# Hybrid decoder layer on one core: four chunks of the second modulation moved to TensorE, a fifth weight slot, a new order of the first loads

## The chip, the cores and the metric

One NeuronCore of a Trainium2 chip runs the whole kernel. The metric is the time of one execution on the device in microseconds (us), as the median of several runs. All data is float32.

## What is computed

One decoder layer on 256 tokens of width 2048. Cut to what matters here:

```python
mod = silu(c) @ w_ada + b_ada                     # (2048) @ (2048 x 12288)
sh1, sc1, g1, sh2, sc2, g2 = split(mod, 6)        # six vectors of 2048
h = rmsnorm(x, norm1_g) * (1 + sc1) + sh1         # first modulation
proj = h @ w_in                                   # 2048 x 4928
o_a = hgrn2(proj)                                 # 8 heads of a gated linear recurrence
o_b = latent_attention(proj)                      # 8 heads, rotary key, low-rank q and kv
x = x + g1 * (concat(o_a, o_b) @ w_out)
h2 = rmsnorm(x, norm2_g) * (1 + sc2) + sh2        # second modulation
y = moe(h2)                                       # top-1 of 4 groups, top-2 of 8 experts, 32 experts
x = x + g2 * y
```

Per expert the weights are 12 MB (gate and up 8 MB, down 4 MB), so the 32 experts are about 403 MB of the 575 MB that a run moves. The six modulation vectors come from one row vector times a 100 MB matrix.

## The kernel before

**The weight stream.** All large weights are cut into chunks of up to 2 MB (128 partitions x 4096 floats). A list `items`, written out in lines 104 to 133, fixes their order, and `ring_fill` (L165) issues their loads in that order on one queue, SyncE's (L174). A chunk takes a slot of a ring; `ring_done` (L183) gives the slot back when the chunk's last reader is done, and only then can the next load go out. The ring has 4 slots (`RING`, L21). Two more are added by `close_temps` (L847, after the second `w_out` chunk of the first half, when the temporaries of the mixers are no longer needed), and one more after the last `w_out` chunk (L892). So 7 chunks at most are loaded ahead of the experts.

**The first modulation.** The vector `c` is copied to all partitions by TensorE (L233, a one-row matmul per 512 columns), passed through sigmoid on ScalarE (L235) and multiplied into `gate` on VectorE (L238). The modulation then comes in two ways. In `ad1_chunk` (L248) and `ada_chunk` (L289) TensorE multiplies a chunk with the silu of `c` as a one-column weight (16 records of the profile per chunk, L257 and L299). In `adt_chunk` (L269) VectorE multiplies a transposed chunk with `gate` and sums along the row: two instructions of 128 x 2048 per chunk (L277). The first 512 features of sh1 and sc1 go through `ad1`, the other twelve blocks of 128 features through `adt` (L106).

**The other modulations** are a list `mods` (L107) of 32 chunks: eight each for g1, for `m2` (the first 1024 features of sh2 and sc2) and for g2, all three on TensorE, then eight chunks `at2` on VectorE for the last 1024 features of sh2 and sc2. `SPREAD` (L23) says how many of them follow each of the last 13 steps: five of the input projection and the mixers, four `w_out` chunks of the first half, four of the second. With `EARLY` one comes before that. So 23 lie ahead of the first `w_out` chunk, three follow it (the last of g2 and two of `at2`), and one follows each of the next six chunks.

**Dense products.** `dense` (L414) handles 128 rows of weights at a time: ScalarE rounds them (L421), VectorE takes the remainder (L422), TensorE does 12 matmuls of 256 columns or their equivalent (L429 to L431, L436 to L438). Four buffers (`NSPLIT`) lie between the engines. `w_out` (L571) adds its result into `xt` on VectorE (L581), and loads `xt` itself, on the same queue as the weights (L588). It is a tile of `arena`, which has 14 buffers; the bias row `brow` of g2, the router weights `wr` and `wr2`, and the mixers' results `mhi` and `mlo` lie in the same arena. The bias is added to g2 on VectorE, row by row (L307), and `gate_rows` (L971) spreads the sum over the partitions.

**Router and experts.** After the last `w_out` chunk come the router (L897 to L966, a chain of small operations), the first gather of tokens (L996) and then the 32 experts (L1052 to L1079), six chunks each.

**The order** of the instructions of each engine is made by a planner from the program's order and priorities; `tc.high_priority(-120)` (L276) puts the VectorE modulation back by 120 steps. The loads of SyncE stand in such an order too: the first chunk of `w_ada` goes out ahead of the four loads of `x` (L214). The table loads of ScalarE (L191 and others) follow the order of its functions.

## Time and profile before

| | us |
|---|---|
| median of 3 runs | 1519.31 |
| lowest, highest | 1517.59, 1519.44 |
| the profiled execution | 1516.6 |
| its span, first to last instruction | 1514.8 |

| engine | busy us | share of the span |
|---|---|---|
| TensorE matmuls | 1116.8 | 74% |
| VectorE | 627.1 | 41% |
| ScalarE | 335.9 | 22% |
| DMA, 574.5 MB at a mean of 379 GB/s | | 91% of 16 engines |

The shares mix two stages. Up to about 580 us all engines work on the mixers while the weights come in; from there on the experts run and TensorE, VectorE and ScalarE mostly wait. The rows below are therefore read by stage. Times in them are microseconds from the start of the span; "x4" is a count of instructions; what stands in brackets is the idle time of the engine just before, and what ended it.

### The profile page before, as it was taken

What the parts mean: (1) busy time and instruction counts of PE and PEld (TensorE: products, weight loads), DVE (VectorE), ACT (ScalarE), POOL (GpSimd) and SP (SyncE); (2) the same over time, 40 slices, a digit from 0 to 9 for tenths busy, and PEclk for the clock granted to TensorE, in tenths of its full rate; (3) what the DMA queues carried; (4) which work ended last, traced back from release to release, by engine and by line L of the source; (5) the groups of instructions that cost most, each with busy time, mean ns of one, the idle gap of its engine ahead of it and who ended that gap; (6) DMA issues with size and microseconds to landing.
All of it is one profiled execution on the core that took longest, in us unless ns stands there. A gap on an engine that the chain in (4) does not pass through costs nothing.

```text
span 1514.8 us, 23373 instructions
## 1 busy us (share of the span) xinstructions
PE 1116.8 (74%) x10141; PEld 708.8 (47%) x10141; DVE 627.1 (41%) x1259; ACT 335.9 (22%) x679; POOL 5.2 (0%) x10
## 2 busy tenths in 40 slices
PE   5979999979888899666666566566667656666665
PEld 2867887637568796333323323323423423333222
DVE  6599998758778862220121122112102112112112
ACT  4734446536433343100100100100100100000000
POOL 0000000000000000000000000000000000000000
PEclk7999999999999998888889888878868889878677
DMA  8789796877979966999999999999999999999995
GB/s 351 270 330 356 300 356 248 333 282 300 373 306 390 389 261 275 427 428 426 427 428 426 427 427 428 426 428 426 427 428 427 427 427 427 427 427 427 427 427 230
DMA packets 42965, 574.52 MB, mean 379 GB/s; under 512 B 4838, under 2 KB 5094, under 8 KB 7660
## 3 DMA queue, kind: packets, MB, share of 16 engines
q1 hardware_dynamic: 41472, 570.51, 90.8%
q10 hardware_dynamic: 1388, 2.49, 0.4%
q8 instruction: 81, 1.33, 0.3%
q14 instruction: 24, 0.20, 0.0%
HBM read 570.88 MB, written 2.10 MB: 378 GB/s over the span
## 4 chain that ended last, share of the span: by engine, by line
DMA 48%; PE 37%; DVE 12%; ACT 2%; issue 1%; ACTq 0%; DVEq 0%
DMA wch<-in_w_gu_dram 37%; DMA wch<-in_w_down_dram 10%; PE pgu L1064 6%; PE pcmb L1019 3%; PE pacc L437 3%; PE pacc L438 3%; PE pacc L431 3%; PE pacc L429 3%; PE pacc L430 3%; DVE wch L277 3%; PE pacc L436 3%; PE py L1042 3%; DVE split L422 2%; PE pada L299 2%; PE pgat L996 1%; DVE proj L461 1%
## 5 line engine op out<-in xcount | busy, mean ns | idle before, releaser
L1064 PE MATMUL pgu<-wch,XT 128*32 128x256 f32 x4096 | 317.2, 464 | 201.3 <-DMA wch<-in_w_gu_dram 201.3
L1064 PEld LDWEIGHTS pgu<-wch,XT 128*32 128x32 f32 x4096 | 141.6, 128 | 368.1 <-DMA wch<-in_w_gu_dram 257.9
L1042 PE MATMUL py<-wch,hT 128*32 128x256 f32 x2048 | 163.2, 474 | 79.3 <-DMA wch<-in_w_down_dram 74.8
L1031 DVE TENSOR_TENSOR hid<-sgu,pgu 128x128 f32<-128x128 f32 x32 | 9.2, 288 | 476.3 <-ACT sgu L1029 476.3
L1046 DVE TENSOR_TENSOR Y<-py,gate 32x256 f32<-32x256 f32 x256 | 107.6, 420 | 213.8 <-PE py L1042 211.0
L421 ACT ACTIVATE split<-wch 128x512 fp32r<-128x512 f32 (+2 forms) x248 | 148.6, 614 | 186.5 <-PE pacc L431 81.4
L422 DVE TENSOR_TENSOR split<-wch,split 128x512 fp32r<-128x512 f32 (+2 forms) x248 | 158.4, 666 | 40.8 <-ACT split L421 38.5
L1042 PEld LDWEIGHTS py<-wch,hT 128*32 128x32 f32 x2048 | 77.8, 130 | 153.0 <-DMA wch<-in_w_down_dram 59.6
L1029 ACT ACTIVATE sgu<-pgu 128x128 f32<-128x128 f32 x32 | 8.9, 278 | 606.9 <-PE pgu L1064 606.9
L1001 ACT ACTIVATE XT<-pgat,sh,a 128x128 f32<-128x128 f32 x128 | 48.2, 457 | 224.9 <-PE pgat L996 224.9
L277 DVE SCALAR_TENSOR_TENSOR wch<-wch,gate 128x2048 f32<-128x2048 f32 x40 | 91.3, 2285 | 0.0
L429 PE MATMUL pacc<-mhi,split 128*128 128x256 f32 x256 | 74.2, 291 | 10.5 <-DVE xt L581 7.2
L437 PE MATMUL pacc<-split,hhi 128*128 128x512 f32 (+1 forms) x192 | 75.1, 391 | 5.9 <-DVE split L422 5.9
L431 PE MATMUL pacc<-mhi,split 128*128 128x256 f32 x256 | 73.5, 289 | 7.9 <-DVE split L422 7.9
L429 PE MATMUL pacc<-hhi,split 128*128 128x256 f32 x256 | 72.6, 287 | 7.7 <-ACT hhi L392 7.2
L436 PE MATMUL pacc<-split,hhi 128*128 128x512 f32 (+1 forms) x192 | 72.3, 389 | 3.0 <-ACT split L421 2.6
L430 PE MATMUL pacc<-hlo,split 128*128 128x256 f32 x256 | 73.1, 287 | 1.7 <-DVE hlo L393 1.7
L431 PE MATMUL pacc<-hhi,split 128*128 128x256 f32 x256 | 72.4, 287 | 2.3 <-DVE split L422 2.3
L430 PE MATMUL pacc<-mlo,split 128*128 128x256 f32 x256 | 73.8, 289 | 0.0
L438 PE MATMUL pacc<-split,hlo 128*128 128x512 f32 (+1 forms) x192 | 73.5, 385 | 0.0
L1019 PE MATMUL pcmb<-Y,pwt 128*128 128x512 f32 x128 | 59.2, 605 | 15.5 <-DVE Y L1046 15.5
L996 PEld LDWEIGHTS pgat<-ohr,x 128*128 128x128 f32 x512 | 63.8, 206 | 9.9 <-issue 9.0
(320 smaller groups left out, 1301.4 us busy)
## 6 DMA issues: line engine op xcount, KB each, us to landing
wch<-in_w_gu_dram SPq DMA_DIRECT2D x128, 2048.0 KB, 31.2
wch<-in_w_down_dram SPq DMA_DIRECT2D x64, 2048.0 KB, 31.8
wch<-in_w_ada_dram SPq DMA_DIRECT2D x28, 2048.0 KB, 10.0
wch<-in_w_ada_t_dram SPq DMA_DIRECT2D x20, 2048.0 KB, 9.8
wch<-in_w_in_dram SPq DMA_DIRECT2D x12, 2048.0 KB, 9.1
wch<-in_w_out_dram SPq DMA_DIRECT2D x8, 2048.0 KB, 14.0
wch<-in_w_in_h_dram SPq DMA_DIRECT2D x8, 1024.0 KB, 9.7
wch<-in_w_in_dram SPq DMA_DIRECT2D x3, 1664.0 KB, 6.7
```

What stands on the lines that cost most here:

```text
L277: V.scalar_tensor_tensor(wk, wk, 1.0, gate, op0=OP.mult, op1=OP.mult, accum_out=r[:, k:k + 1])
L421: S.activation(s[:, 0, :ncol], w, AF.Copy)
L422: V.tensor_sub(s[:, 1, :ncol], w, s[:, 0, :ncol])
L429: PE.matmul(o, s[:, 0, c], hi, start=first and h % 2 == 0, stop=False, skip_group_check=True)
L430: PE.matmul(o, s[:, 0, c], lo, start=False, stop=False, skip_group_check=True)
L431: PE.matmul(o, s[:, 1, c], hi, start=False, stop=stop, skip_group_check=True)
L436: PE.matmul(o, hi[:, c], s[:, 0, :ncol], start=first, stop=False)
L437: PE.matmul(o, hi[:, c], s[:, 1, :ncol], start=False, stop=False)
L438: PE.matmul(o, lo[:, c], s[:, 0, :ncol], start=False, stop=stop)
L1042: PE.matmul(py[32 * j:32 * j + 32, :256], H["T"][:, 32 * kt:32 * kt + 32], w[:, 1024 * kt + 256 * j:1024 * kt + 256 * j + 256], start=kt = ...
L1046: V.tensor_mul(Y[q][r:r + 32, 256 * j:256 * j + 256], py[32 * j:32 * j + 32, :256], gate[32 * j:32 * j + 32, c:c + 256])
L1064: PE.matmul(gu[32 * j:32 * j + 32, :256], XT[G4][kt // 8][:, kt % 8, 32 * e4:32 * e4 + 32], w[:, 1024 * i + 256 * j:1024 * i + 256 * j + 2 ...
```

## The change

- The ring gets a fifth slot (`RING` 5). The room comes from the call that builds the program, which sets `dynamic_dma_scratch_size=1024`.
- Four of the eight `at2` chunks (8 to 11) become four chunks `m3`: the same 512 features of sh2 and sc2, not transposed, multiplied on TensorE in the way of `ada_chunk`, eight matmuls per chunk. After the fourth, ScalarE copies the sums to `rows`, four small matmuls with two selecting columns (`C_SEL`) turn them into columns, and VectorE adds bias and gain for four blocks at once. In `mods` the `m3` chunks stand between `m2` and g2.
- `SPREAD` changes: 25 chunks instead of 23 lie ahead of the first `w_out` chunk, the three that follow it are of g2, and one `at2` chunk follows each of the next four `w_out` chunks. The last three have none. `router_weights(2)` runs after `m3`, so its buffer is taken earlier.
- The remaining `at2` chunks are put back by 20 steps instead of 120.
- The first load of the ring is ordered behind the last load of `x`; five chunks are requested before the constants instead of three.
- `c` and the bias of g2 are rows of one array; `c` is loaded in one transfer instead of two, onto four partitions, and its four one-row matmuls use different row groups of the array. The positions travel with `pcol`, which saves a transfer. `brow` leaves the arena, and its load goes out later.
- The two exponentials of `forget_bound` are ordered behind the load of the logarithm and exponential tables.
- g2 is copied by one ScalarE instruction; the bias is added in `gate_rows` by a second one-row matmul, so there are eight of them instead of four.

The core of the diff:

```diff
-RING, NARENA, NTEMP, NSPLIT, RING2 = 4, 14, (8, 6), 4, 2
-SPREAD = (1, 4, 7, 5, 5, 3, 1, 1, 1, 1, 1, 1, 0)
+RING, NARENA, NTEMP, NSPLIT, RING2 = 5, 14, (8, 6), 4, 2
+SPREAD = (1, 4, 7, 6, 6, 3, 1, 1, 1, 1, 0, 0, 0)
...
-    pos_i = cpool.tile([P, 2], I32, name="pos_i")
     nc.sync.dma_start(pc, A["pcol"])
-    nc.sync.dma_start(pos_i, A["pos"])
...
-    mods = [("ada", b, ch) for b in ("g1", "m2", "g2") for ch in range(8)] + [("at2", kt) for kt in range(8, 16)]
+    mods = [("ada", b, ch) for b, n in (("g1", 8), ("m2", 8), ("m3", 4), ("g2", 8)) for ch in range(n)]
+    mods += [("at2", kt) for kt in range(12, 16)]
...
-            nc.sync.dma_start(t[:, :cols], src)
+            load = nc.sync.dma_start(t[:, :cols], src)
+            if i == 0:
+                in_order(load, ring["behind"])
...
-    crow = tmp([1, 1024], "crow"), tmp([1, 1024], "crow")
-    for h in range(2):
-        nc.scalar.dma_start(crow[h], A["crow"][:, 1024 * h:1024 * h + 1024])
+    crow = big([P, 512], "crow")
+    nc.scalar.dma_start(crow[0:128:32], A["rows"][:, 0])
...
-        nc.sync.dma_start(xx[j], A["xT"][:, 4 * j:4 * j + 4])
-    ring["limit"] = 3
+        x_load = nc.sync.dma_start(xx[j], A["xT"][:, 4 * j:4 * j + 4])
+    ring["behind"] = x_load
+    ring["limit"] = 5
     ring_fill()
-    brow = big([P, 512], "brow")
-    nc.scalar.dma_start(brow[0:128:32], A["b_g"])
     nc.sync.dma_start(cst, A["cst"])
...
-        PE.matmul(ps, one_row, crow[h // 2][:, 512 * (h % 2):512 * (h % 2) + 512], start=True, stop=True)
+        PE.matmul(ps, ones[32 * h:32 * h + 1, :], crow[32 * h:32 * h + 1], start=True, stop=True, tile_position=(32 * h, 0))
...
-            with tc.high_priority(-120):
+            with tc.high_priority(-120 if it[0] == "adt" else -20):
...
+        if b == "m3":
+            for i in range(4):
+                kt = 4 * ch + i
+                for m in range(2):
+                    j, o = 2 * (i % 2) + m, 1024 * i + 512 * m
+                    PE.matmul(acc[b][32 * j:32 * j + 1, :], ca[:, kt:kt + 1], w[:, o:o + 512], start=kt < 2, stop=kt >= 14)
+            ring_done(("ada", b, ch))
+            if ch == 3:
+                S.activation(rows, acc[b], AF.Copy)
+                ps = pm("pcol3")
+                for n in range(4):
+                    PE.matmul(ps[:, 2 * n:2 * n + 2], rows[:, 128 * n:128 * n + 128], cst[:, C_SEL:C_SEL + 2], start=True, stop=True)
+                t = sm(8, "m3")
+                V.tensor_copy(t, ps[:, 0:8])
+                t2 = t.rearrange("p (n b) -> p b n", b=2)
+                mod_shift(sh2[:, 8:12], t2[:, 0], P_BA + 32 + 8, 4)
+                mod_scale(a2[:, 8:12], t2[:, 1], P_BA + 48 + 8, P_N2 + 8, 4)
+            return
...
         if b == "g2":
-            for j in range(4):
-                V.tensor_add(brow[32 * j:32 * j + 1], brow[32 * j:32 * j + 1], acc[b][32 * j:32 * j + 1])
+            S.activation(g2row, acc[b], AF.Copy)
             return
...
-        S.activation(e0, e0, AF.Exp)
-        S.activation(e1, e1, AF.Exp)
+        in_order(S.activation(e0, e0, AF.Exp), tables)
+        in_order(S.activation(e1, e1, AF.Exp), tables)
...
-        ("at2", 11): lambda: router_weights(2),
+        ("ada", "m3", 3): lambda: router_weights(2),
...
-            PE.matmul(ps, ones[32 * j:32 * j + 1, :], brow[32 * j:32 * j + 1], start=True, stop=True, tile_position=(32 * j, 0))
+            for row in (g2row, brow):
+                PE.matmul(ps, ones[32 * j:32 * j + 1, :], row[32 * j:32 * j + 1], start=row is g2row, stop=row is brow,
+                          tile_position=(32 * j, 0))
...
-    nc = bacc.Bacc("TRN2", target_bir_lowering=False, num_devices=1)
+    nc = bacc.Bacc("TRN2", target_bir_lowering=False, num_devices=1, dynamic_dma_scratch_size=1024)
```

## Rows read from the trace of the kernel before

**Rows 1.** The page's head: the span.
```profile
span 1514.8 us, 23373 instructions
```

**Rows 2.** Windows by stage: each engine's busy time (count), granted clock, DMA share, GB/s.
```profile
40.00:240.00 200.00, 184.05 (x1100) 153.44 (x1098) 176.47 (x294) 100.92 (x183) 0.00 (x0) 0.99 0.83 316
240.00:433.00 193.00, 177.91 (x1205) 120.01 (x1205) 141.77 (x293) 98.56 (x188) 2.87 (x3) 0.96 0.76 300
433.00:560.00 127.00, 108.62 (x879) 105.81 (x876) 102.86 (x178) 43.41 (x69) 0.95 (x1) 0.93 0.89 364
560.00:580.00 20.00, 16.55 (x116) 13.68 (x116) 8.54 (x48) 10.03 (x27) 0.00 (x0) 0.74 0.23 93
580.00:1500.00 920.00, 601.57 (x6727) 302.57 (x6727) 166.44 (x378) 64.25 (x185) 0.00 (x0) 0.84 1.00 423
```

**Rows 3.** Timeline of SyncE's queue, 510 to 590: start, duration of the merged stretch, load, count.
```profile
510.74 28.33 SPq L174 DMA_DIRECT2D wch<-in_w_gu_dram  x4
539.16 13.26 SPq L174 DMA_DIRECT2D wch<-in_w_down_dram  x2
556.40 31.56 SPq L174 DMA_DIRECT2D wch<-in_w_gu_dram  x4
```

**Rows 4.** Chain that ended last: start, duration, what; the first and the last expert load.
```profile
578.01 1.86 PE pgu L1064 x32
...
1458.04 30.81 DMA wch<-in_w_gu_dram
```

**Rows 5.** Windows of three shorter stretches, columns as in rows 2.
```profile
40.00:60.00 20.00, 20.00 (x129) 14.65 (x128) 8.46 (x15) 14.59 (x25) 0.00 (x0) 1.00 0.55 181
450.00:460.00 10.00, 2.86 (x12) 2.57 (x13) 9.79 (x21) 2.19 (x4) 0.00 (x0) 0.54 0.99 418
1000.00:1200.00 200.00, 132.72 (x1445) 65.31 (x1437) 35.63 (x78) 12.93 (x38) 0.00 (x0) 0.83 1.01 427
```

**Rows 6.** Timeline of the start, and the four one-row matmuls of `gate_rows` at 563.90.
```profile
2.54 7.16 PE L233 MATMUL pc<-crow,one_row 1*128 1x512 f32 x8 [2.54 <-DMA crow<-in_crow_dram]
...
10.16 1.28 ACT L235 ACT_TABLE_LOAD   x1
...
12.07 1.28 ACT L191 ACT_TABLE_LOAD   x1
13.36 2.00 ACT L327 ACTIVATE sq<-x 128x1024 f32<-128x1024 f32 x2
...
34.33 0.80 PE L429 MATMUL pacc<-hhi,split 128*128 128x256 f32 x2 [7.01 <-ACT hhi L392]
...
563.90 2.27 PE L975 MATMUL pg<-brow,ones 1*128 1x512 f32 x8
```

**Rows 7.** Timeline of VectorE: the first `adt` instruction of the run.
```profile
66.46 2.29 DVE L277 SCALAR_TENSOR_TENSOR wch<-wch,gate 128x2048 f32<-128x2048 f32 x1
```

**Rows 8.** Timeline of ScalarE: its three longest waits for a weight chunk.
```profile
214.57 2.19 ACT L421 ACTIVATE split<-wch 128x512 fp32r<-128x512 f32 x4 [5.06 <-DMA wch<-in_w_in_dram]
...
281.93 2.19 ACT L421 ACTIVATE split<-wch 128x512 fp32r<-128x512 f32 x4 [4.62 <-DMA wch<-in_w_in_dram]
...
450.11 2.19 ACT L421 ACTIVATE split<-wch 128x512 fp32r<-128x512 f32 x4 [9.09 <-DMA wch<-in_w_out_dram]
```

**Rows 9.** Timeline: one TensorE modulation chunk; the bias additions; two successive weight splits.
```profile
445.67 1.90 PE L299 MATMUL pada<-wch,ca 128*1 128x512 f32 x16
447.63 2.78 DVE L307 TENSOR_TENSOR brow<-brow,pada 1x512 f32<-1x512 f32 x4 [1.32 <-PE pada L299]
...
547.92 0.63 ACT L421 ACTIVATE split<-wch 128x512 fp32r<-128x512 f32 x1 [0.79 <-PE pacc L431]
549.35 0.63 ACT L421 ACTIVATE split<-wch 128x512 fp32r<-128x512 f32 x1 [0.79 <-PE pacc L431]
```

**Rows 10.** Groups by line: the VectorE modulation, all 20 chunks.
```profile
L277 DVE SCALAR_TENSOR_TENSOR wch<-wch,gate 128x2048 f32<-128x2048 f32 x40 | 91.3, 2285 | 0.0
```

**Rows 11.** Waits of SyncE's queue up to 620: the loads of `xt`.
```profile
SPq L588 <- PE pacc L431: 6.2, 1, 6.2
```

More of the change, by code (lines that the diff above doesn't have):

```diff
@@ L31 @@
 NEG = -3.0e38
-C_ID, C_TRI64, C_TRI, C_MASK, C_IOTA, C_IOTM, C_FREQ, C_RESET = (
-    0, 128, 256, 384, 640, 672, 704, 736)
-C_W = 992
+C_ID, C_TRI64, C_TRI, C_MASK, C_IOTA, C_IOTM, C_FREQ, C_RESET, C_SEL = (
+    0, 128, 256, 384, 640, 672, 704, 736, 992)
+C_W = 994
 P_C, P_N1, P_N2, P_QA, P_KVA, P_QN, P_KN, P_HO, P_AO, P_LB, P_BA = (
     0, 16, 32, 48, 52, 54, 55, 56, 57, 58, 74)
-P_W = 154
+P_POS = 154
+P_W = 156
 R_QPE, R_KPE, R_B = 0, 64, 128
@@ L133, in tile_hybrid_layer, with in_order, log_exp_tables @@
     index = {it: i for i, it in enumerate(items)}
+    def in_order(inst, before):
+        tc.add_manual_dep(inst.ins, before.ins.name, mybir.DependencyInfo(mybir.DependencyClass.NoSync, mybir.DependencyReason.DATA),
+                          reason="order")
+    def log_exp_tables(inst):
+        load = S.preload_act_table_set("natural_log_exp_and_others")
+        in_order(load, inst)
+        return load
     def source(it):
@@ L145, in source @@
         if k == "ada":
+            if it[1] == "m3":
+                return A["w_ada_3"][it[2]], 4096
             return A["w_ada"][("g1", "m2", "g2").index(it[1]), it[2]], 4096
         if k == "at2":
-            return A["w_ada_t2"][it[1] - 8], 4096
+            return A["w_ada_t2"][it[1] - 12], 4096
         if k == "win":
@@ L186, in ring_done @@
         ring_fill()
-    def log_exp_tables(inst):
-        load = S.preload_act_table_set("natural_log_exp_and_others")
-        tc.add_manual_dep(load.ins, inst.ins.name, mybir.DependencyInfo(mybir.DependencyClass.NoSync, mybir.DependencyReason.DATA),
-                          reason="tables")
     def rsqrt(ms, n):
@@ L228, in tile_hybrid_layer @@
     V.tensor_mul(ca, ca, cin)
-    one_row = cpool.tile([1, P], F32, name="one_row")
-    V.memset(one_row, 1.0)
     for h in range(4):
         ps = pm("pc")
-        PE.matmul(ps, one_row, crow[h // 2][:, 512 * (h % 2):512 * (h % 2) + 512], start=True, stop=True)
+        PE.matmul(ps, ones[32 * h:32 * h + 1, :], crow[32 * h:32 * h + 1], start=True, stop=True, tile_position=(32 * h, 0))
         g = gate[:, 512 * h:512 * h + 512]
@@ L236, in tile_hybrid_layer @@
         if h == 3:
-            log_exp_tables(i)
+            tables = log_exp_tables(i)
         V.tensor_mul(g, g, ps)
+    brow = cpool.tile([P, 512], F32, name="brow")
+    S.dma_start(brow[0:128:32], A["rows"][:, 1])
     acc = {}
     rows = cpool.tile([P, 512], F32, name="rows")
+    g2row = cpool.tile([P, 512], F32, name="g2row")
     sh1 = cpool.tile([P, 16], F32, name="sh1")
@@ L1173, in _layout @@
     sh1, sc1, g1, sh2, sc2, g2 = range(6)
-    L["pcol"] = ac(np.concatenate([L["pcol"]] + [col(ba[k]) for k in (sh1, sc1, sh2, sc2, g1)], axis=1))
-    L["crow"] = np.asarray(i["c"]).reshape(1, D)
-    L["b_g"] = ac(ba[g2].reshape(4, 512))
+    L["pcol"] = ac(np.concatenate([L["pcol"]] + [col(ba[k]) for k in (sh1, sc1, sh2, sc2, g1)]
+                              + [ac(np.asarray(i["positions"])[0].reshape(2, P).T).view(np.float32)], axis=1))
+    L["rows"] = ac(np.stack([np.asarray(i["c"]).reshape(4, 512), ba[g2].reshape(4, 512)], axis=1))
     wt = lambda b: wa[:, :, b].reshape(D, 16, P).transpose(1, 2, 0)
     L["w_ada_t"] = np.stack([wt(sh1), wt(sc1)], axis=2).reshape(16, P, 4096)[4:]
-    L["w_ada_t2"] = np.stack([wt(sh2), wt(sc2)], axis=2).reshape(16, P, 4096)[8:]
+    L["w_ada_t2"] = np.stack([wt(sh2), wt(sc2)], axis=2).reshape(16, P, 4096)[12:]
+    t = np.stack([wa[:, :, b, 1024:1536].reshape(4, 4, P, 512) for b in (sh2, sc2)], axis=3)
+    L["w_ada_3"] = ac(t.transpose(0, 2, 1, 3, 4)).reshape(4, P, 4096)
     t = np.stack([wa[:, :, b, :512].reshape(2, 8, P, 2, 256) for b in (sh1, sc1)], axis=4)
```

4 lines of the change are left out of this document (2 added, 2 removed).

## The prediction

> **What bounds the kernel now.** I read the windows by stage first, because the page's shares mix two programs. From about 580 us to the end the DMA engines are busy all the time at 423 GB/s on average (427 in the middle), while TensorE works 602 of 920 us and VectorE 166 [rows 2, 5]. So the end is set by a stream of weights at a constant rate, and the only question is when that stream begins and how much is already loaded by then. SyncE's queue answers the second: four gate-up chunks and two down chunks go out up to 552, one more at 556.40, and then the queue has no slot [rows 3]; between 560 and 580 the DMA share is 0.23 [rows 2]. So seven chunks are loaded when the first expert chunk is used up, at 578.01 + 1.86 = 579.9 [rows 4]. There are 32 x 6 = 192 chunks of 2.097 MB; the other 185 take 2.097 / 0.427 = 4.91 us each [rows 5], 908.4 us together, which gives 1488.3. The last gate-up load landed at 1458.04 + 30.81 = 1488.9 [rows 4]. The rest, to 1514.8, is a tail that the change leaves alone [rows 1]. The formula therefore holds:
>
> span = (time T1 at which the first expert chunk is used up) + 4.91 x (192 - chunks loaded by then) + 26.5
>
> Up to T1 the engines set the pace. From 40 to 240 both TensorE (184 of 200) and VectorE (176) are nearly full, from 240 to 433 TensorE is (178 of 193), and DMA has a share of 0.83 and 0.76 [rows 2]. From 433 to 560, the `w_out` stage, TensorE works 109 of 127 us, VectorE 103, and DMA's share rises to 0.89 [rows 2]: nothing is full there, the three wait for each other.
>
> **The change part by part**, against the profiled execution (1516.6; its span 1514.8).
>
> *Fifth slot, after T1: -4.9.* Eight chunks loaded instead of seven. It counts in full only if the eighth can land before T1; between 560 and 580 the DMA engines are idle for 0.77 x 20 = 15.4 us [rows 2], so a T1 that is earlier by some 10 us does not take that away (the w_out stage would also have fewer bytes, since two modulation chunks leave it). This term I hold for the surest. The Trainium skill ("DMA: Bandwidth & Descriptors", Specifications) gives a core's limit from HBM as about 358 GB/s. The window at 427 contradicts it for this core [rows 5]; by the page's figure a slot would be an estimated 5.9 us instead of 4.9. The measurement decides.
>
> *The start: -5.0.* ScalarE's squares of `x` begin at 13.36, and the first dense matmul starts at 34.33 after a chain through them [rows 6]. Ahead of the squares stand the four one-row matmuls (7.16 us) and two table loads of 1.28 that the new order saves: one back to the sigmoid at 10.16, one forth again at 12.07 [rows 6]. Tables alone give 2.6. Four one-row matmuls in different row groups exist in this trace, in `gate_rows`: 2.27 us instead of 7.16 [rows 6], so at most 4.9 more. Together 2.6 to 7.5; I take the middle, since sigmoids still follow one another on ScalarE. `x` in front of the first 2 MB chunk lands up to 4.9 us earlier, so it doesn't hold the squares. The chunk now lands later, but what the first dense step needs is `x` and the first two chunks of `w_ada`, 6.3 MB in either order, 14.7 us of transfer at 427: both orders have it by about 20 us, before the chain through `x` is done. The saved transfers of a few KB are worth nothing visible: cover is the 2 MB behind them.
>
> *40 to 240: -4.0.* From 40 to 60 TensorE is full and VectorE works 8.5 of 20 us [rows 5], because the first `adt` chunk is only there at 66.46 [rows 7]; afterwards VectorE is almost the bound (176 of 200). One more slot brings that chunk one load earlier, so one chunk's VectorE work, 2 x 2.285 = 4.6 us [rows 10], can move into the idle time. ScalarE's wait of 5.06 at 214.57 for a chunk [rows 8] may go too. Bounds: nothing (TensorE goes on as the bound) to 8, half of TensorE's idle 16 us in this stretch [rows 2].
>
> *240 to 433: +2.0.* Two more modulation chunks lie ahead of `w_out`: 2 x 1.90 = 3.8 us of TensorE [rows 9], and the end of `m3`, a copy and small operations, that I put at 1 us from the copy of 128 x 512 at 0.63 that ScalarE does in the splits [rows 9]. TensorE is idle 15 us of this stretch [rows 2], and the wait of 4.62 at 281.93 for a chunk [rows 8] may disappear with a deeper ring. Bounds +4.8 to -4.6; I take +2 since the idle pieces lie in dependent chains which only partly admit a filler.
>
> *433 to 560: -11.5.* TensorE needs 64 splits' worth of matmuls at 549.35 - 547.92 = 1.43 us [rows 9], 91.5 us. Lost are 127 - 108.6 = 18.4 us of idle time, and, with a granted clock of 0.93 on average, that is about 18 us at the lower of the two levels (1.2 instead of 2.4 GHz), I estimate some 5 us of slow matmuls after the idle pieces [rows 2]. The largest piece is 450 to 460: 7.1 us idle, clock 0.54, VectorE full [rows 5]. Three things meet there: ScalarE waited 9.09 us for the second `w_out` chunk [rows 8], VectorE did the bias rows for 2.78 us [rows 9], and two `at2` chunks of 2 x 2.285 us each [rows 10]. All three go: the slot loads the chunk earlier, ScalarE copies g2, and three g2 chunks stand in place of one and two `at2`. I count 7.1 + 2.5 for this. The other 11.3 us of idle time I put down to VectorE, which at one `at2` chunk per `w_out` chunk has 4.6 for it, 8 splits that I put at ScalarE's 0.63 each [rows 9], and the additions to `xt`: 9.7 and more, against TensorE's 8 x 1.43 = 11.4, with little room for an instruction at the wrong place; with eight `at2` chunks cut to four, half of it goes, 5.6. Two further g2 chunks cost 3.8 of TensorE. 7.1 + 2.5 + 5.6 - 3.8 = 11.4. Bounds: 3.3 (only the 7.1 less the 3.8) to 19 (18.4 + 5 less 3.8). The later place of the remaining `at2` chunks, 20 steps back instead of 120, has no row; I give it nothing, with up to 2.3 us either way, one instruction ahead of a split.
>
> *560 to T1: 0.* `gate_rows` gets four more matmuls, 2.3 us by its row [rows 6]; they stand while the router's small operations run, where TensorE is idle 3.45 of 20 us [rows 2]. Without that cover they cost 2.3.
>
> Sum: -4.9 - 5.0 - 4.0 + 2.0 - 11.5 = -23.4; T1 comes at about 561. 1516.6 - 23.4 = 1493.2. The profiled execution lies 2.7 below the median of the runs shown, so the median should be 1496.
>
> **The rivals.**
>
> *The start is swallowed.* From 60 to 240 VectorE's work is fixed (176 of 200 us busy), and it begins when the first `adt` chunk lands. If the load order, not the start of the dense steps, sets that moment, then -5 and -4 both end in TensorE waiting for VectorE: 1496 + 9 = 1505. For it: VectorE's load in rows 2. Against it: loads wait for slots there (share 0.55 from 40 to 60 [rows 5]), and an earlier first step frees them earlier.
>
> *VectorE goes on setting the pace in the w_out stage.* Four chunks still need 2 x 2.285 each there, beside splits that TensorE needs every 1.43; if the order keeps an `at2` in front of the splits each time, only the piece at 450 returns, 3.3 instead of 11.5: 1504.
>
> *More is gained.* If TensorE runs without a gap in the w_out stage (-19) and 40 to 240 gives 8, then 1496 - 7.5 - 4 = 1484.5.
>
> *Only the slot counts.* The saved VectorE time is idle time elsewhere and the added chunks cost 4.8: 1516.6 - 4.9 + 4.8, by the median about 1519.
>
> *Slower: the arena blocks the load queue.* SyncE's queue is strictly in order; in the kernel before, the load of the fourth `xt` held it for 6.2 us until a `w_out` matmul was done [rows 11]. By my count 14 buffers were full then: eight of mixer results, `brow`, `wr`, one `wr2` and three `xt`; the change takes `brow` out but fetches the second `wr2` before `w_out` begins, so it again reaches 14 with the third `xt`. If one more tile is alive than I count, two further loads of `xt` wait, each for about one `w_out` chunk (11.4 us), with all weight loads behind them: +22.8, and the gain of 11.5 in that stage is gone as well. 1496 + 22.8 + 11.5 = 1530. It decides as soon as the second `xt` finds no buffer; only its count of 13 speaks against it.
>
> **How the numbers follow.** Forecast 0.52, with a range of its own from 1489 to 1503. Start swallowed 0.16; VectorE goes on 0.14; more gained 0.08; only the slot 0.04; slower 0.06. All but the last two, and these near the edges of what the bounds allow, lie between 1482 and 1511: the upper end is 1496 + 9 + 8, less 2 because both misses in full are unlikely together, the lower end that of the third rival with 2.5 for the start's upper bound. What a measurement of this kernel can tell from no change is about 0.2%, 3 us. Faster: 0.52 + 0.16 + 0.14 + 0.08 = 0.90; same 0.04; slower 0.06.
>
> **What would show it.** The stream after T1 still at 427 with eight chunks requested before T1, T1 at 561; squares beginning near 8 to 9 and the first dense matmul near 29; the first `adt` before 60; `w_out` beginning near 426 and its stage 115 us long, without ScalarE's wait of 9 us and without a low clock at its start; no wait of an `xt` load over 6 us. It would be wrong if DMA never idles before T1 (then the slot is worth nothing), if TensorE waits for `adt` after 200, or if a modulation chunk keeps TensorE waiting for its load between 380 and 430.

## The result and the profile after

| | before | after |
|---|---|---|
| median, us | 1519.31 | 1527.34 |
| lowest, highest | 1517.59, 1520.07 | 1525.05, 1529.43 |
| the profiled execution, its span | 1516.6, 1514.8 | 1527.34, 1525.1 |

The changed kernel is slower by about half a per cent: the ratio of the times is 1.0055, with a 95% interval from 1.0039 to 1.0071. The forecast was 1496, and faster.

The windows by stage of the changed kernel, columns as in rows 2 (busy time and count of TensorE, weight load, VectorE, ScalarE, GpSimd; granted clock; DMA share; GB/s):

```profile
40.00:240.00 200.00, 184.67 (x1091) 156.78 (x1093) 176.85 (x300) 100.41 (x174) 0.00 (x0) 0.97 0.81 313
240.00:433.00 193.00, 171.25 (x1158) 118.26 (x1150) 142.08 (x298) 100.25 (x196) 3.76 (x4) 0.97 0.75 296
433.00:560.00 127.00, 113.12 (x911) 99.95 (x910) 81.22 (x147) 45.08 (x72) 0.00 (x0) 0.95 0.88 364
560.00:580.00 20.00, 18.02 (x147) 16.89 (x145) 9.99 (x41) 8.62 (x22) 0.00 (x0) 0.95 0.57 211
580.00:1500.00 920.00, 603.56 (x6743) 306.43 (x6746) 166.07 (x387) 67.79 (x194) 0.00 (x0) 0.84 0.99 419
...
1000.00:1200.00 200.00, 127.64 (x1440) 63.25 (x1432) 37.81 (x83) 12.35 (x36) 0.00 (x0) 0.86 1.01 427
```

VectorE was relieved between 433 and 560 as planned (81.2 us instead of 102.9 [rows 2]), and the experts' stream is the same as before, 427 GB/s in the middle (the last line, and rows 5). But from 240 to 433, where more work was to be done, TensorE did less, 171.3 instead of 177.9. So the kernel had fallen behind there, and that is where to look.

Four points of the trace, in us from the span's start, place the loss. A split is the preparation of 128 weight rows, rounded on ScalarE and the remainder taken on VectorE; on VectorE the 185th is the first of `w_out`, the 248th is the last; T1 is the end of the first expert chunk, in the changed kernel this line of TensorE's timeline:

```profile
592.95 1.93 PE L1091 MATMUL pgu<-wch,XT 128*32 128x256 f32 x32
```

| | before | after | difference |
|---|---|---|---|
| 169th split | 352.6 | 352.0 | -0.6 |
| first `w_out` split | 431.7 | 445.2 | +13.5 |
| last `w_out` split | 551.4 | 562.7 | +11.3 |
| T1 | 579.9 | 594.9 | +15.0 |
| span | 1514.8 | 1525.1 | +10.3 |

Up to 352 the two kernels are level. Some 14 us are lost from there to the first `w_out` split, 2 come back in the `w_out` stage, nearly 4 are lost in the router, and the fifth slot returns 5 behind T1.

SyncE's queue shows the first of these losses. Each line is the start of a stretch, its length and the chunks requested in it; first the kernel before, then the changed one:

```profile
376.52 0.33 SPq L174 DMA_DIRECT2D wch<-in_w_in_dram  x1
...
409.02 0.33 SPq L174 DMA_DIRECT2D wch<-in_w_out_dram  x1
```

```profile
339.12 31.14 SPq L187 DMA_DIRECT2D wch<-in_w_ada_dram  x5
377.12 0.33 SPq L187 DMA_DIRECT2D wch<-in_w_in_dram  x1
382.42 30.86 SPq L187 DMA_DIRECT2D wch<-in_w_ada_dram  x6
436.53 0.33 SPq L187 DMA_DIRECT2D wch<-in_w_out_dram  x1
```

The first load of `w_out` goes out at 436.53; in the kernel before it went out at 409.02. The queue isn't short of bandwidth: in the window from 420 to 430 the DMA engines are idle (DMA share 0.01; before, 0.27).

```profile
420.00:430.00 10.00, 9.57 (x59) 7.07 (x60) 6.08 (x13) 1.83 (x4) 0.95 (x1) 0.77 0.01 2
```

It waits for slots that modulation chunks hold. These are the queue's waits for a modulation matmul (sum, count, longest), up to 620 in the kernel before and up to 640 in the changed one:

```profile
SPq L174 <- PE pada L299: 142.0, 24, 20.3
```

```profile
SPq L187 <- PE pada L325: 128.0, 23, 23.2
...
SPq L613 <- PE pacc L456: 9.6, 1, 9.6
```

The sum didn't grow, and a wait of some 20 us for matmuls behind the recurrence stood in the queue before too, from 411.1 to 431.4. But it held up the two `at2` chunks then, with `w_out`'s first load already out; with two more chunks ahead it holds up `w_out`'s load itself, from 413.3 to 436.5.

The `w_in` load, by contrast, is only 0.6 us later than before (377.12 against 376.52), and it has landed at 386.13. Yet ScalarE rounds that chunk's first 128 rows 10 us later than before. First the kernel before, then the changed one, where the attention's last exponentials (L842) stand ahead:

```profile
385.48 2.19 ACT L421 ACTIVATE split<-wch 128x512 fp32r<-128x512 f32 x4 [0.68 <-DMA wch<-in_w_in_dram]
```

```profile
391.73 0.51 ACT L842 ACTIVATE s<-s,sm 128x256 f32<-128x256 f32 x1 [6.18 <-DVE sm L840]
...
395.62 0.61 ACT L446 ACTIVATE split<-wch 128x512 fp32r<-128x512 f32 x1
```

So at this place it is the planner's order, and not the date of the load, that differs from the kernel before. In the waits above, the last line is the load of `xt`, of which my slower rival spoke: one wait, 9.6 instead of 6.2 [rows 11], not three.

### The profile page after: what moved, and what is told of

Its sections match the earlier page's. It is cut to its first block, busy times and chain, and to the rows that moved or that the text cites. A ratio compares the mean times of both kernels' runs of the same rounds, so it can differ in the third digit from the quotient of the medians.

```text
span 1525.1 us, 23510 instructions
## 1 busy us (share of the span) xinstructions
PE 1125.5 (74%) x10221; PEld 714.7 (47%) x10221; DVE 607.4 (40%) x1231; ACT 337.1 (22%) x681; POOL 5.1 (0%) x10
## 5 line engine op out<-in xcount | busy, mean ns | idle before, releaser
L454 PE MATMUL pacc<-mhi,split 128*128 128x256 f32 x256 | 74.5, 291 | 13.3 <-DVE xt L606 10.3
L285 DVE SCALAR_TENSOR_TENSOR wch<-wch,gate 128x2048 f32<-128x2048 f32 x32 | 72.9, 2283 | 0.0
L1023 PEld LDWEIGHTS pgat<-ohr,x 128*128 128x128 f32 x512 | 62.7, 203 | 11.1 <-issue 11.1
```

The lines of the kernel that those rows point to most:

```text
L285: V.scalar_tensor_tensor(wk, wk, 1.0, gate, op0=OP.mult, op1=OP.mult, accum_out=r[:, k:k + 1])
L454: PE.matmul(o, s[:, 0, c], hi, start=first and h % 2 == 0, stop=False, skip_group_check=True)
```

## The experiments

All runs were compared with runs of the kernel before on the same chip, in five rounds. "T1" and the splits are read in each run's profiled execution, and one such execution can lie up to 6.6 us from its kernel's median (the start alone: 1526.96 against 1520.39); the verdicts go by the ratios.

### Taking the change apart

**Only the fifth slot**, the rest as before:

```diff
-RING, NARENA, NTEMP, NSPLIT, RING2 = 4, 14, (8, 6), 4, 2
+RING, NARENA, NTEMP, NSPLIT, RING2 = 5, 14, (8, 6), 4, 2
-    nc = bacc.Bacc("TRN2", target_bir_lowering=False, num_devices=1)
+    nc = bacc.Bacc("TRN2", target_bir_lowering=False, num_devices=1, dynamic_dma_scratch_size=1024)
```

> The kernel before with the fifth slot alone. Theory A (the slot is worth one chunk of the stream and no more, 4.9 us; the loss of the whole change comes from the four m3 chunks and their place): about 1514.5. Rival B (more loads ahead change the planner's order so that modulation chunks come before the second recurrence's matmuls, whatever m3 does): the first expert chunk is used up later than at 580, and the time is 1519 or more.

1511.03 us, ratio 0.9945 (0.9927 to 0.9963): a gain of 8 us by the median. Theory A gave the slot 4.9; my sum had 4.9 for it behind T1 and, with the earlier `adt` chunk, 4.0 ahead of it.

**The changed kernel with four slots** (`RING` 4):

> The changed kernel with four slots again. Theory A: the stream starts with seven chunks instead of eight, +4.9 us, 1532. Rival B (the slot itself lets modulation chunks crowd in front of w_out): the w_out stage begins earlier than at 445 and the time is below 1527.

1540.15 us, 1.0134 (1.0112 to 1.0156): without the slot all the rest costs 20 us, and the slot is worth 13 in the changed kernel. That is more than either theory said.

**Only the new start**: the order of `x` and `w_ada`, `c` on four partitions, the table loads, the positions in `pcol`, five requests ahead of the constants.

> The kernel before with the new start alone: x ahead of w_ada, c in one transfer and row groups, exponentials behind the table load, positions with pcol. My prediction: 5 us less, 1514. Theory A (TensorE has the first modulation chunk's matmuls, which wait for the later landing of that chunk, between the two matmuls of the square sums): the first dense matmul 1 to 2 us earlier, nothing left of it at 240, within 2 us of 1519.

1520.39 us, 1.0017 (1.0007 to 1.0027): worth nothing, rather a little less than that.

**No `m3`**: the changed kernel with all eight `at2` chunks and the old `SPREAD`; slot, start and `g2row` stay.

```diff
-    mods = [("ada", b, ch) for b, n in (("g1", 8), ("m2", 8), ("m3", 4), ("g2", 8)) for ch in range(n)]
-    mods += [("at2", kt) for kt in range(12, 16)]
+    mods = [("ada", b, ch) for b, n in (("g1", 8), ("m2", 8), ("g2", 8)) for ch in range(n)]
+    mods += [("at2", kt) for kt in range(8, 16)]
-SPREAD = (1, 4, 7, 6, 6, 3, 1, 1, 1, 1, 0, 0, 0)
+SPREAD = (1, 4, 7, 5, 5, 3, 1, 1, 1, 1, 1, 1, 0)
...
```

> The changed kernel without m3: eight at2 chunks on VectorE and SPREAD as in the kernel before; the slot, the start and the g2 row stay as changed. Theory A (m3 and the two further chunks ahead of w_out cost more than VectorE's relief gives): 1512 to 1516, that is the slot alone (1511) plus about 4 for the eight one-row matmuls, less up to 1.5 for the start. Rival E (the loss comes from the start or from another part kept here): 1523 or more.

1510.69 us, 0.9958 (0.9945 to 0.9970); first `w_out` split at 430.5. So the loss comes with `m3` or with the two chunks that `SPREAD` puts ahead of `w_out`, and without them hardly anything is left but the slot's gain.

### `m3`, or the two chunks ahead of `w_out`?

Two kernels complete the square. The first is the changed kernel with the old `SPREAD` (23 chunks ahead) and `m3`:

> The changed kernel with the old SPREAD alone: the four m3 chunks stay, and 23 modulation chunks stand ahead of w_out instead of 25, two more behind it. Theory E (the two extra chunks, which hold the slots while w_out's loads should start, cost the time): first w_out split 445 -> 431 to 434, last logits matmul at 553 to 557, median 1510 to 1515. Theory F (the m3 chunks themselves cost it, by the planner's order of TensorE's queue and the clearing of the one accumulator): first w_out split not before 440, median 1520 to 1526.

The second has no `m3`, but the new `SPREAD` (25 ahead):

> The opposite half: no m3 chunk (eight VectorE chunks at2, as before), but 25 modulation chunks ahead of w_out as in the changed kernel. The fifth slot, the new start and g2row stay. Theory E: first w_out split at 440 to 446, later than the 430.5 of the kernel without m3 and with 23; median 1518 to 1527. Theory F: first w_out split near 432, median 1510 to 1513.

| median, us (ratio) | 23 ahead of `w_out` | 25 ahead |
|---|---|---|
| eight `at2` | 1510.69 (0.9958) | 1535.16 (1.0115) |
| four `m3`, four `at2` | 1511.99 (0.9962) | 1527.34 (1.0055) |

With 23 chunks it makes no difference whether the four chunks run on TensorE or on VectorE. With 25 both kernels lose, by 15 and 24 us, the one without `m3` more than either theory had expected. So the loss comes with the `SPREAD` line, with or without `m3`. SyncE's queue of the kernel with `m3` and 23 chunks shows the other course:

```profile
337.21 27.82 SPq L187 DMA_DIRECT2D wch<-in_w_ada_dram  x4
368.03 0.33 SPq L187 DMA_DIRECT2D wch<-in_w_in_dram  x1
375.23 26.57 SPq L187 DMA_DIRECT2D wch<-in_w_ada_dram  x5
407.38 0.33 SPq L187 DMA_DIRECT2D wch<-in_w_out_dram  x1
```

One modulation chunk fewer stands ahead of the last `w_in` chunk, which goes out 9.1 us earlier (368.03 instead of 377.12), and one fewer ahead of `w_out`, which goes out 29 us earlier. The recurrence of the last heads needs that `w_in` chunk, and here ScalarE rounds its first rows at 383.56, ahead of the last exponentials (390.31), as in the kernel before. Its first matmuls, L549, in this kernel and then in the changed one (TensorE's timeline):

```profile
415.88 1.94 PE L549 MATMUL ptr<-cst,d 128*128 128x128 f32 x8 [6.84 <-DVE d L542]
428.52 5.33 PE L325 MATMUL pada<-wch,ca 128*1 128x512 f32 x48
435.74 1.06 PE L592 MATMUL pmt<-cst,o 128*128 128x128 f32 x8
```

```profile
420.43 1.86 PE L325 MATMUL pada<-wch,ca 128*1 128x512 f32 x2 [7.54 <-ACT d L537]
422.22 1.97 PE L549 MATMUL ptr<-cst,d 128*128 128x128 f32 x8
...
434.59 6.19 PE L325 MATMUL pada<-wch,ca 128*1 128x512 f32 x56
440.86 1.06 PE L592 MATMUL pmt<-cst,o 128*128 128x128 f32 x8
```

Seen from L592, the mixer's last result, the changed kernel is 5.1 us behind (and 1.8 behind the kernel before, 439.10); at the last split it is 14.3 behind (562.7 against 548.4). What differs most is the work done ahead of that result: eight splits of `w_out` had begun on ScalarE ahead of it in the kernel before and five with `m3` and 23 chunks, but none in the changed kernel.

The kernel without `m3` loses by another course. Its `w_out` load goes out at 414.47, 22 us earlier than in the changed kernel, and its first `w_out` split still comes at 445.7. The 25th chunk is an `at2` chunk there, and VectorE runs its two instructions (at 437.98 and 440.26) ahead of the mixer's last large operations, which began at 438.24 in the changed kernel (L585). L592, which waits for them, starts at 445.96:

```profile
414.47 0.33 SPq L187 DMA_DIRECT2D wch<-in_w_out_dram  x1
```

```profile
437.98 2.28 DVE L285 SCALAR_TENSOR_TENSOR wch<-wch,gate 128x2048 f32<-128x2048 f32 x1
...
443.33 1.23 DVE L585 TENSOR_TENSOR o<-o,sm 128x1024 f32<-128x1024 f32 x1
```

A late load of `w_out` is thus not needed for the loss.

### Number, place, or bytes?

**24 chunks**: `SPREAD` (1, 4, 7, 5, 6, 3, 1, 1, 1, 1, 1, 0, 0), one of the two extra chunks, behind the last `w_in` load.

> The changed kernel with 24 modulation chunks ahead of w_out: five ahead of the last two heads' w_in load, as with 23, and six between that load and w_out's first, as in the changed kernel. Theory E1 (each of the two extra chunks costs by its own place): w_in's load is issued near 368, as with 23, w_out's first load later than 407; first w_out split between 430 and 440, median 1514 to 1522. Theory E2 (only the chunk ahead of the w_in load hurts, since it moves the recurrence): median 1511 to 1514. Theory E3 (only the chunk just ahead of w_out hurts): 1523 to 1528.

1517.99 us, 0.9997 (0.9988 to 1.0005). The `w_in` load is issued at 368.57 and L549 starts at 416.42, as with 23; the last `w_out` split comes at 552.4. So this one chunk costs 6 us by the median, and the other, ahead of the `w_in` load, 9: 1512.0, 1518.0, 1527.3 (5 and 9 by the ratios).

**25 chunks, the extra two early**: (1, 6, 7, 5, 5, 3, 1, 1, 1, 1, 0, 0, 0).

> The changed kernel with 25 chunks ahead of w_out, but the two extra ones right behind the first group of the third mixer (1, 6, 7, 5, 5) instead of around its last w_in load. If the place decides, the last part runs as with 23 chunks: first w_out split at 425 to 432, median 1510 to 1515. If the number decides (two chunks, 9.8 us of stream, ahead of everything that follows), first w_out split at 437 to 447 and median 1520 to 1528.

1533.66 us, 1.0107 (1.0092 to 1.0122), beyond both expectations. An earlier place is no cure, it is worse: the last `w_in` load goes out at 378.59, L549 starts at 427.29, the first `w_out` split at 450.3.

**Fewer ahead of `w_out`**: (1, 4, 7, 6, 3, 3, 2, 2, 1, 1, 1, 0, 0), 22 chunks, but still six ahead of the last `w_in` load.

> The changed kernel with three modulation chunks fewer ahead of w_out: SPREAD (1, 4, 7, 6, 3, 3, 2, 2, 1, 1, 1, 0, 0). Theory A (six chunks in a row hold all five slots, so the first w_out load goes out at 436 instead of 409, the DMA engines stand still from 420 to 437, and the w_out stage then runs behind the stream): the first w_out load goes out 10 to 20 us earlier, the stage ends 8 to 12 us earlier, 1516 to 1519. Rival C (what counts is TensorE's wait of 7.5 us at 413 to 420 for a cleared accumulator): that wait stays, and the time stays within 3 us of 1527.

1516.32 us, 0.998 (0.997 to 0.999). Three chunks were moved behind `w_out`'s start, and 11 us came back; the first `w_out` split is at 422.1 and the stage from there to the last is 130 us long instead of 117.5. The mixer's last result comes at 440.68, as late as in the changed kernel (440.86), but five splits of `w_out` had begun on ScalarE ahead of it; so the lateness of the mixer is not what cost these 11 us. In the kernel with the slot alone, one chunk fewer (`SPREAD` (1, 4, 7, 5, 4, 3, 2, 1, 1, 1, 1, 1, 0)) was no help either:

> The kernel before with the fifth slot alone and one modulation chunk fewer ahead of w_out (22). The kernel with the slot alone took 1511.0 with 23. If 23 already delays w_out's first load, 22 gives a further 2 to 5 us (1506 to 1509); if the stage behind is then limited by the stream, the chunk costs there what it saves here: 1510 to 1513.

1514.58 us, 0.9975 (0.9964 to 0.9986), against 1511.03 with 23, above both values that were expected. Its profiled execution, 1508.94, was the fastest of seven, which is why the median is used. Of the numbers tried, 23 is the best.

**The bytes away**: the first five g2 chunks load 512 of their 4096 columns.

```diff
+            if it[1] == "g2" and it[2] < 5:
+                return A["w_ada"][2, it[2]][:, :512], 512
             return A["w_ada"][("g1", "m2", "g2").index(it[1]), it[2]], 4096
...
-                o = D * k + 512 * j
+                o = 0 if b == "g2" and ch < 5 else D * k + 512 * j
```

> The changed kernel in which the first five g2 chunks, those that stand ahead of w_out's first load, bring only 512 of their 4096 columns each, and their matmuls use these 512 throughout: the same instructions, slots and order, 5 x 7/8 x 2.097 MB = 9.2 MB less to load, 21.5 us of the stream at 427 GB/s; most of the gate's values are others. Theory S (the chunks cost through the slots that they hold until TensorE's queue reaches them, behind the recurrence): w_out's first load is issued at 430 to 437, first w_out split at 441 to 446, median 1523 to 1528. Rival B (they cost through their bytes): w_out's first load before 420, first w_out split before 432, median under 1513.

1529.93 us, 1.0067 (1.0048 to 1.0086). SyncE's queue and two windows of this kernel:

```profile
377.65 0.33 SPq L189 DMA_DIRECT2D wch<-in_w_in_dram  x1
...
437.11 0.33 SPq L189 DMA_DIRECT2D wch<-in_w_out_dram  x1
```

```profile
400.00:410.00 10.00, 9.25 (x64) 8.37 (x64) 8.70 (x17) 8.15 (x11) 0.00 (x0) 1.00 0.06 19
410.00:420.00 10.00, 3.42 (x30) 1.70 (x28) 10.00 (x24) 4.02 (x5) 0.00 (x0) 0.92 0.10 34
```

The median is 2 us above what either theory gave. The DMA engines stand nearly still (0.06 and 0.10), yet the `w_in` and the `w_out` load go out within 0.6 us of the changed kernel's, and nothing is gained. The extra chunks don't cost bytes; they cost their places: in the load queue, where `w_out`'s load waits for a slot and the slot for a matmul behind the recurrence, and, as the kernel without `m3` showed, in the engines' queues.

### One wait after the other

**The accumulator cleared by ScalarE.** The 7.54 us that TensorE waits at 420.43 end with VectorE's clearing of the one accumulator, from 419.84 to 420.32, which stands behind the recurrence's operations (the view names L537, which ended earlier, at 420.04). Here g2's accumulator is cleared by ScalarE.

```diff
-            V.memset(acc[b], 0.0)
+            if b == "g2":
+                S.activation(acc[b], cst[:, 0:512], AF.Copy, scale=0.0)
+            else:
+                V.memset(acc[b], 0.0)
```

> The changed kernel, with the accumulator of g2 cleared by ScalarE instead of VectorE, where the clearing stands behind five large operations of the recurrence. Rival C: TensorE's wait of 7.5 us goes, the recurrence's transposes start near 416 instead of 422, and the time falls by 5 to 7 us, to 1521. Theory A: the wait goes, but the loads of w_out come little earlier because the same six chunks stand ahead of them; the time falls by 3 us or less.

1527.16 us, 1.0061 (1.0042 to 1.0081): no gain. The wait fell to 1.35 us, slots came free earlier and `w_out`'s first load went out at 414.45 instead of 436.53, which Theory A had not expected. The recurrence gained little: its first matmuls came at 420.45 instead of 422.22, now behind a wait of 3.50 for VectorE. But ScalarE splits the chunk only when its queue comes to it, and there the split stands behind the mixer's last result (L501 is the changed kernel's L498):

```profile
441.40 1.27 ACT L501 ACTIVATE mhi<-pmt,pc 128x512 fp32r<-128x512 f32 x2 [4.14 <-PE pmt L595]
442.56 2.19 ACT L449 ACTIVATE split<-wch 128x512 fp32r<-128x512 f32 x4
```

In the kernel with `m3` and 23 chunks, splits of `w_out` stand ahead of it:

```profile
430.20 1.14 ACT L446 ACTIVATE split<-wch 128x512 fp32r<-128x512 f32 x2
...
436.40 1.27 ACT L498 ACTIVATE mhi<-pmt,pc 128x512 fp32r<-128x512 f32 x2 [0.26 <-PE pmt L592]
```

So a late load is not the whole cause here either: the planner's order has also put `w_out`'s first splits behind the mixer. In the changed kernel itself the first split waits only 1.75 us for its load, from 442.80 to 444.55.

**The `at2` chunks put back by 120 steps again** (instead of 20):

> The changed kernel with all VectorE modulation put back by 120 steps, the four at2 chunks too. Theory A (the w_out stage follows its loads, which go out late): within 3 us of 1527. Rival D (put back by 20 steps only, two at2 chunks run one after the other ahead of an xt addition at 507 to 512, and TensorE waits 8.3 us for it): the wait goes and the time falls by 6 to 8 us, to 1520.

1526.10 us, 1.0056 (1.0043 to 1.0069): no effect. But Rival D was not put to the test: the two `at2` instructions stand one after the other ahead of the addition to `xt` as they did (506.60 and 508.81, the addition at 511.80), and TensorE still waits 8.35 us for it.

**VectorE's additions in the slot's kernel**: one addition of the whole accumulator to a cleared `brow` instead of four rows.

> The kernel before with the fifth slot and, in the w_out stage, one VectorE addition of the whole accumulator to brow instead of four additions of a row each (brow cleared first on GpSimd). My prediction gave VectorE's time in the w_out stage a worth. If VectorE sets the pace there, 1 to 2 us less than 1511.0; if not, 1510.5 to 1511.5.

1510.17 us, 0.9947 (0.9932 to 0.9962), against 0.9945 with four: 2 us less on VectorE in the `w_out` stage are worth nothing.

**Half of the `at2` loads.** The four `at2` chunks, all in the `w_out` stage, load half their columns, and VectorE does the same work.

```diff
-            return A["w_ada_t2"][it[1] - 12], 4096
+            return A["w_ada_t2"][it[1] - 12][:, :2048], 2048
...
-            wk = w[:, 2048 * k:2048 * k + 2048]
+            wk = w[:, 2048 * k:2048 * k + 2048] if it[0] == "adt" else w[:, :2048]
```

> The changed kernel in which each of the four at2 chunks, all in the w_out stage, loads only its first 2048 columns, which VectorE multiplies twice: the same instructions, 4 MiB less to load in that stage, and half of those modulation values are others. One chunk of 2 MiB takes 4.91 us in the steady stream, so 9.8 us of transfer are taken out. Theory (the stream is the bound between the first w_out split and the first expert chunk): last VectorE split 562.7 -> 551 to 555 and median 1515 to 1519. Rival (VectorE or TensorE sets the pace there): last split within 3 us of 562.7, median 1524 to 1528.

The total, 3066 us, can't be read, which I hadn't foreseen: the other modulation values change the routing, and the router falls into the path for too many tokens per expert, which loads all experts' weights again (975 MB instead of 574.5). Up to 560 the trace can be read: the last split comes at 556.7, between the two expectations. Of 9.8 us of transfer 6.0 came back, 1.1 of it ahead of the first `w_out` split (1.0 already at the 113th split, long before the edit acts), so the stream sets part of this stage and not all of it. In the changed kernel the DMA share is 1.01 from 445 to 520; from 540 TensorE is full:

```profile
445.00:460.00 15.00, 15.00 (x127) 12.24 (x128) 5.64 (x11) 4.27 (x8) 0.00 (x0) 1.00 1.01 430
460.00:480.00 20.00, 16.97 (x131) 14.76 (x124) 13.07 (x23) 7.73 (x13) 0.00 (x0) 0.91 1.01 426
480.00:500.00 20.00, 18.05 (x139) 17.88 (x139) 14.84 (x26) 7.21 (x12) 0.00 (x0) 0.91 1.01 425
500.00:520.00 20.00, 11.65 (x88) 11.48 (x87) 15.69 (x28) 4.57 (x8) 0.00 (x0) 0.83 1.01 426
...
540.00:560.00 20.00, 20.00 (x169) 19.67 (x169) 13.78 (x23) 9.24 (x14) 0.00 (x0) 1.00 0.46 176
```

### The router, and a candidate

**Four gate matmuls again**: GpSimd clears `brow`, VectorE adds it to `g2row` in one instruction.

```diff
...
             S.activation(g2row, acc[b], AF.Copy)
+            V.tensor_add(g2row, g2row, brow)
...
-            for row in (g2row, brow):
-                PE.matmul(ps, ones[32 * j:32 * j + 1, :], row[32 * j:32 * j + 1], start=row is g2row, stop=row is brow, ...)
+            PE.matmul(ps, ones[32 * j:32 * j + 1, :], g2row[32 * j:32 * j + 1], start=True, stop=True, tile_position=(32 * j, 0))
```

> The changed kernel with the bias of g2 added by one VectorE instruction again, and four one-row matmuls in gate_rows instead of eight. Theory A (the extra matmuls stand in TensorE's queue in front of the router's transposes and the first gather, and cost about 4 us there): from the last w_out matmul to the first expert chunk 21 to 22 us instead of 25; the time falls by 3 to 5 us, to 1523. Rival (they lie beside the router's small operations): within 1 us of 1527.

1524.26 us, 1.0047 (1.0032 to 1.0062); by the ratios 0.0008, some 1 us, better than the changed kernel, with intervals that overlap. Its trace has the 3.8 us: from the last logits matmul to T1 it takes 21.4 instead of 25.2. In the changed kernel the bias's one-row matmuls stand in TensorE's queue ahead of the router's own (L986) and of the gather (L1023):

```profile
580.84 2.07 PE L1001 MATMUL pg<-brow,ones 1*128 1x512 f32 x2
582.84 0.37 PE L986 MATMUL prm<-cst,sm 128*1 128x128 f32 x1
583.14 2.07 PE L1001 MATMUL pg<-g2row,ones 1*128 1x512 f32 x2
585.01 1.91 PE L1001 MATMUL pg<-brow,ones 1*128 1x512 f32 x2
586.85 6.17 PE L1023 MATMUL pgat<-ohr,x 128*128 128x128 f32 x32
```

With it, without `m3` and with 23 chunks:

> The candidate: the changed kernel without m3, with 23 chunks ahead of w_out, and with the bias added to g2row by one VectorE instruction, so that gate_rows has four matmuls instead of eight. Against the kernel without m3 (1510.7) the router's chain should be 3 to 4 us shorter: median 1507 to 1509. If that chain is covered by the loads, no difference: 1510 to 1511.

1511.92 us, 0.9959 (0.9947 to 0.9971): no better than without it (0.9958). The fastest kernels are all the same to within their intervals, 0.9945 to 0.9962: the slot alone, the slot with one addition, and the changed kernel with 23 chunks ahead of `w_out`, with or without `m3`.

## Why the prediction was wrong

By the spans, 1525.1 came where 1491.4 was forecast (1514.8 - 23.4). Of these 33.7 us, 8.4 were missing by the 169th split (-0.6 where the start and 40 to 240 had been booked with -9), 12.1 from there to the first `w_out` split, 9.3 in the `w_out` stage and 3.7 in the router. Behind T1 the forecast held to 0.2.

**The formula: right.** span = T1 + 4.91 x (192 - chunks loaded) + 26.5 gives 594.9 + 903.4 + 26.5 = 1524.8 for the changed kernel; its span was 1525.1. With four slots (T1 604.6, seven chunks) it gives 1539.4 against 1538.4, with `m3` and 23 chunks (579.5) 1509.4 against 1508.6, with the early 25 (600.5) 1530.4 against 1530.6. The largest miss is the kernel with 22 chunks and six ahead of `w_in`: 1514.3 against 1517.5. The slot's -4.9 behind T1 held. Alone the slot is worth 8, near the 4.9 and 4.0 that I had booked for it, and in the changed kernel 13. By the figure of the Trainium skill ("DMA: Bandwidth & Descriptors", Specifications), about 358 GB/s for each of the two cores that share a stack, a chunk would take an estimated 5.9 us. Here one core runs the kernel, and the window from 1000 to 1200 after the change again has 427.

**The start, -5: wrong.** The pieces came at least as large as priced, and none reached the end. The squares began at 5.33 instead of 13.36, the one-row matmuls took 2.08 for three of four, the table loads were gone. But TensorE's queue had this order:

```profile
16.73 1.19 PE L361 MATMUL pss<-sq,ones 128*128 128x256 f32 x2 [7.01 <-DVE lbc L434]
17.85 3.59 PE L265 MATMUL pad<-wch,ca 128*1 128x512 f32 x16
21.37 0.87 PE L361 MATMUL pss<-sq,ones 128*128 128x256 f32 x2
...
32.89 0.80 PE L454 MATMUL pacc<-hhi,split 128*128 128x256 f32 x2 [7.05 <-ACT hhi L417]
```

A modulation chunk of 16 records stands between the two halves of the sum of squares (L361), so the second half began at 21.37, where in the kernel before the whole sum began at 21.15. The first dense matmul came at 32.89 instead of 34.33 [rows 6], and at the ninth split the kernels were level (45.9 and 45.6). The step "both orders have it by about 20 us, before the chain through `x` is done" failed: the later chunk took a place inside that chain in TensorE's queue. This is my rival of the swallowed start, by another mechanism than the one I gave it.

**40 to 240, -4: wrong.** The first `adt` instruction came at 66.08 instead of 66.46 [rows 7]; with the slot alone it came at 63.74. At the 113th split the slot alone was 2.0 us ahead of before (215.0 against 217.0), the start alone 4.7 behind (221.7, in its longest execution), the changed kernel 3.7 behind. The three kernels with five slots and the old start had it at 215.0 to 216.0, the thirteen with five slots and the new start at 217.3 to 221.3: the new start took away more than the slot brought.

**240 to 433, +2.0: the step that failed most.** The first `w_out` split came 13.5 us later than before, although the changed kernel was 0.6 ahead at 352. I priced two chunks as 3.8 us of TensorE work. What they cost is their places: with 23 of them ahead the first split came at 427.4, 4.3 earlier than before, with 25 at 445.2. By the medians it is 15.4 us for the two (14 by the ratios). I had named a modulation chunk that waits for its load as the sign of this. What happened is that the load of `w_out` waited for a slot, a chunk for its accumulator, and that splits of the last `w_in` chunk and of `w_out` took later places on ScalarE.

**433 to 560, -11.5: wrong.** From the first to the last split the stage took 119.7 us before and 117.5 after. The signs that I had read did go: ScalarE's 9.09 us wait for the second `w_out` chunk is 1.69, and the granted clock from 450 to 460 is 1.00 instead of 0.54 [rows 5]. The step that failed was to add these idle pieces up as if each were a loss of its own. They moved:

```profile
507.53 2.28 DVE L285 SCALAR_TENSOR_TENSOR wch<-wch,gate 128x2048 f32<-128x2048 f32 x1
...
509.74 2.29 DVE L285 SCALAR_TENSOR_TENSOR wch<-wch,gate 128x2048 f32<-128x2048 f32 x1
...
512.73 1.65 DVE L606 SCALAR_TENSOR_TENSOR xt<-pacc,g,xt 128x256 f32<-128x256 f32 x4
```

```profile
513.74 0.55 PE L454 MATMUL pacc<-mhi,split 128*128 128x256 f32 x1 [8.35 <-DVE xt L606]
```

Two `at2` instructions stand on VectorE ahead of the additions to `xt`, and TensorE waits 8.35 us for these. Where the number of chunks is the same, taking four `at2` chunks off VectorE made the stage longer, not shorter: 121.0 us with `m3`, 115.8 without, both with 23 (the first split is 3.1 us earlier with `m3`, the last 2.1 later). A likely reason, which no run isolates, is that in `mods` each `m3` chunk pushes one of g2 behind `w_out`'s start, so the stage has five g2 chunks on TensorE instead of one. And the stream is full from 445 to 520, as the windows above show; I had read the DMA share of 0.89 [rows 2] as not full.

**560 to T1, 0: wrong by the amount I had put on it.** The cover for the four matmuls was gone, as their place in the queue shows; I put 2.3 on that case, and from the last logits matmul to T1 it took 3.7 more (25.2 against 21.6). Three of them ran there one by one, at 2.07, 2.07 and 1.91.

**The rivals.** The slower rival, `xt` loads held by the arena, didn't happen (one wait of 9.6 us). That the range ended below 1519 is the same mistake as the forecast: I had allowed the two added chunks at most 4.8 us, TensorE's work and no more, and so no slower case but that one.

**What stays open.** That the two chunks' places cost the time is shown; how the loss of 15 us divides between the late loads and the changed order on ScalarE, VectorE and TensorE isn't settled. Two kernels with 25 chunks, the ScalarE-cleared one and the one without `m3`, had the `w_out` load out 22 us earlier than the changed kernel without a gain, but their order was not that of the kernel with 23 chunks, and an order was not set by hand in any run. Why the planner chose these orders the traces don't show.

## What to carry to other kernels

A filler that is put ahead of a chunk in one ring of slots can cost more than its work on the engine, here 15 us for 3.8 us of matmuls: it holds a slot, it can delay the loads that follow, and the matmuls that free the slot may stand behind a dependent chain. It can also change the planner's order on every engine, with the loads on time. So price a moved item by the dates of the loads behind it and by what the engines do ahead of the next dependent result, and try each number of fillers with the work itself unchanged. Idle time that several causes share is worth no more than the next resource allows: in a stage with the DMA share at 1.01 for 75 us, relieving VectorE gave nothing.

## What was unexpected of the hardware

One-row matmuls of 1 x 512 (two records each) ran side by side where they used different row groups. At the start of the changed kernel three together took 2.08 us (at 2.94) and the fourth, alone, 2.07 (at 7.65), at a granted clock of 1.00 from 2 to 10; four together took 2.31 in the router of the kernel with four gate matmuls; four in one row group took 7.16 [rows 6]. So the price of `gate_rows` hangs on the order: I had priced eight at 2 x 2.27, and in the changed kernel five in one stretch took 2.19 (from 575.25), while the three that the planner had scattered among the router's matmuls took 2.07, 2.07 and 1.91 one by one. The granted clock was 0.50 there (580 to 590), the lower of the two levels (1.2 GHz), after TensorE had stood idle for 1.98 us before the router's ranks at 579.42; but one alone took the same 2.07 at either level.
